# The low half of a weight block, split before or after the background work of its slot

## The chip, the cores and the metric

The kernel runs on one core of one Trainium2 chip. The metric is the device time of one execution in microseconds, from the first to the last instruction of the core and the little that lies around it. The core has five engines with a queue each: TensorE (PE; its weight loads are shown as PEld), VectorE (DVE), ScalarE (ACT), GpSimd (POOL) and SyncE (SP, which here issues the weight transfers).

## The reference

One decoder step in float32, for 512 prompt positions and 8 x 8 sampled ones, 576 rows in all. Attention, convolution and the output projection come first; what the change touches is the MLP and the gate behind them:

```python
    x = x + jnp.concatenate([attn, conv_y], axis=-1) @ w_out
    hid = jnp.square(jax.nn.relu(rms_norm(x, g_mlp) @ w_up))      # 2048 -> 8192
    x = x + hid @ w_down                                          # 8192 -> 2048
    gate = jax.nn.sigmoid(rms_norm(x, g_ple) @ w_ple_gate)        # 2048 -> 2048
    return x + (pe @ w_ple) * gate
```

## The kernel before

**Numbers.** Every float32 operand is split into a high half, rounded to TensorE's fast float32 form, and a low half, the rest. ScalarE makes the high half (`split_hi`, L163), VectorE then the low one from the operand and the high half (`split_lo`, L166). A product is three matmuls: high weights by high rows (L1692), high by low (L1693), low by high (L1694).

**Blocks.** The second phase (`phase2`, from about 963 us on) works through weight blocks, called quads: 2 x 2 tiles of 128 x 128 weights against 2 x 2 tiles of 128 x 288 row operands. In up (256 quads, 32 output pairs p of 8) and down (256 quads, in segments of mostly 7) a quad is not done with 8 tile products but with 7, after Strassen's scheme: three sums of the weights (VectorE, L1918 to L1920) give 7 weight rows, three sums of the row operands (`tsums`, L1778 to L1781, the tile T) give 7 operand rows, and `PRODS` says which weight row meets which operand row for which of the 7 results q0 to q6. So a quad is 7 x 3 = 21 matmuls of 288 columns. The gate (120 quads, `plain`, L1762 to L1764) uses plain products.

**A slot of the loop.** The loop over quads (L1660 to L1723) writes, for quad t, in this order: the second part of the previous segment's end (`combine_tail`, L1817 ff.: VectorE takes the results out of PSUM), `W.prep(t + 2)` (`QStream.prep`: the high split of the block after the next on ScalarE, one pending weight sum, its low split, one more sum), the 21 matmuls, then the background. In the last quad of a segment there is no general background; `combine_head` stands there instead (L1803 ff.: q0 and q4 are copied by ScalarE at L1810 and L1813, then L1811 and L1812 on VectorE use up q5 and q6).

**Background.** Generators wait in queues: `fin_up` (squares the finished up rows: L1447 on VectorE, L1450 and L1451 on ScalarE), `operands` and `tsums` (T), `low_rows` (splits of rows for down, tile lr), `slot` (splits of the next row operands, tile xs: two high splits on ScalarE, two low ones on VectorE), and the gate's end (`fin_gate`, L1500 and L1502). `bg.run(t, dt)` adds an allowance dt of VectorE time and runs steps until it is used up; `bg.wait` only adds it; `flush` runs an item to its end where it is needed. All this happens when the program is written: on the chip each engine runs its queue in the order written.

**What ties the engines.** There are 3 buffers of split weights (w2hl), so the high split of quad t + 2 waits for TensorE to end quad t - 1. There are 4 buffers of raw weights (w2r, two quads each); SyncE's transfer into one waits for the last low split that read it. The 8 PSUM banks turn round: the fourth product of a new segment takes the bank that L1811 frees.

Of the kernel before, what the change touches and what calls it, by code (L numbers as in the profile page):

```python
# [13 lines left out]
ALU = mybir.AluOpType  # L14
# [6 lines left out]
HR = 288  # L21
# [65 lines left out]
def f(ap):  # L87
    return ap.bitcast(F32)


def braid(t, sets=4):
    return t.rearrange("p (b a c) -> p a b c", a=sets, c=4)


def both(t):
    return t[..., 0], t[..., 1]


class Shift:


    def __init__(self, t, off):
        self.t, self.off = t, off
# [6 lines left out]
def EL(n):  # L110

    return n / 960.0 + 0.07


class WStream:
# [24 lines left out]
    def low(self):  # L140
        for c in sorted(set(self.raw) & set(self.hl)):
            hi, lo = self.hl[c]
            self.nc.vector.tensor_tensor(lo, self.raw.pop(c), f(hi), ALU.subtract)  # L143
# [13 lines left out]
class Kern:  # L157
# [1090 lines left out]
    def outproj(self, gen):  # L1248

        nc, a = self.nc, self.a  # L1250
        self.open2()
        bg, t2 = self.bg, self.t2
        for n in range(KT):
            self.on = n
            if n % 2 == 0:
                if n >= 4:
                    bg.flush(self.fin_of[0, n // 2 - 2])
                self.oc_ = t2.tile([128, 2, NR], F32, name="c", tag="c", bufs=3)
            self.rx = self.w2.tile([128, NR], F32, name="rx", tag="t5", bufs=1)
            nc.sync.dma_start(self.rx, a["x"][:, n, :])  # L1260
            h = 6 if n == 0 else 0
            for _ in gen:
                bg.spend(EL(512) / 2)
                if n == KT - 4 and h == 0:
                    for i in range(4):
                        self.W.dma(i)
                if n == KT - 3 and h % 2:
                    bg.spend(self.W.ahead(h // 2))
                if n == KT - 1 and h in (2, 4, 6):
                    bg.spend(self.W.prep(h // 2 - 1))  # L1270
                bg.run(8 * n + h, 1.6)
                h += 1
            if n % 2 and n < KT - 1:
                self.fin_of[0, n // 2] = bg.add(0, self.fin_out(n // 2, self.oc_))
            gen = self.gemm_tile(self.out_evac if n < KT - 2 else self.last_evac)
# [5 lines left out]

    PRODS = ((0, 2, 0), (6, 5, 5), (5, 6, 4), (4, 4, 3), (2, 0, 2), (1, 3, 1), (3, 1, 6))

    def open2(self):

# [144 lines left out]
    def phase2(self):  # L1432
# [11 lines left out]
        V = nc.vector.tensor_tensor  # L1444
# [25 lines left out]
        def rows_of(g):  # L1470
            return {3: (0, 1), 4: (0,), 5: (1,)}[g]
# [81 lines left out]
        segs, W, slots, fin_of = self.segs, self.W, self.slots, self.fin_of  # L1553
# [67 lines left out]
        for n in range(RING, len(seq)):  # L1621
            g, j = seq[n]
# [37 lines left out]
        for t, (si, k) in enumerate(quadlist):  # L1660
            g, p, *_ = segs[si]
            ks = self.orders[si]
            n, i = len(ks), t - seg0[si]
            if prev:
                pg, ppr, c, r, pfinal, pp_ = prev
                if pg >= 3:
                    cost = self.plain_end(ppr, c, rb)
                else:
                    cost = self.combine_tail(ppr, EL)
                    c = c[0]  # L1670
                bg.spend(cost)
                late = (pg, pp_) == (1, 31)
                fin_of[pg, pp_] = bg.add(2 if late else 0, fins[pg](pp_, c, r, pg if pg >= 3 else pfinal))
                if not late:
                    recent.append(fin_of[pg, pp_])
                prev = None
            s = slots[min(g, 3), k]
            if s.work is not None:
                bg.flush(s.work)
                s = slots[min(g, 3), k]  # L1680
            bg.spend(W.prep(t + 2))
            hi, lo = W.hl.pop(t)
            if i == 0:
                pr = {}
            if g >= 3:
                self.plain(pr, hi, lo, s, i == 0, i == n - 1, rows_of(g))
            else:
                for (q, ia, ib) in self.PRODS:
                    if i == 0:
                        pr[q] = self.P_()  # L1690
                    o, xh, xl = braid(pr[q][:, :HR]), braid(s.hi[:, ib, :]), braid(s.lo[:, ib, :])
                    nc.tensor.matmul(o, hi[:, ia, :], xh, start=(i == 0), stop=False)  # L1692
                    nc.tensor.matmul(o, hi[:, ia, :], xl, start=False, stop=False)  # L1693
                    nc.tensor.matmul(o, lo[:, ia, :], xh, start=False, stop=(i == n - 1))  # L1694
            for fn in hooks.get(t, ()):
                fn()
            if g == 2 and p in (4, 5, 6) and i in (0, 2):
                bg.nudge(2)
            slow = p == 0 and g != 2
            if i == (n - 2 if g < 4 else 5) and not slow:  # L1700
                if g > 1:
                    bg.flush_all(0)
                r = pre[g](p, lastseg[g, p] == si)
            dt = (2.79, 3.18, 1.59, 1.59)[max(g - 2, 0)]
            if i == n - 1:
                bg.wait(1000 + t, dt)
            else:
                bg.run(1000 + t, dt)
            if g == 1 and p == 0 and i + 2 < n and slots[1, ks[i + 2]].work:
                bg.flush(slots[1, ks[i + 2]].work)  # L1710
            if i == n - 1:
                if g > 1:
                    bg.flush_all(0)
                if slow:
                    r = pre[g](p, lastseg[g, p] == si)
                if recent[0]:
                    bg.flush(recent[0])
                if g >= 3:
                    c = t2.tile([128, 2, NR], F32, name="c", tag="c", bufs=3)
                else:  # L1720
                    c = self.combine_head(pr, cx if (g, p) == (1, 31) else None)
                    bg.spend(2 * EL(HR))
                prev = (g, pr, c, r, lastseg[g, p] == si, p)  # L1723
# [3 lines left out]
        pg, ppr, c, r, pfinal, p = prev  # L1727
        c, acc = c[:, :, :HR], self.acc2[:, HR:]
# [44 lines left out]
    def tsums(self, T, c):  # L1773

        V = self.nc.vector.tensor_tensor
        b21, b22 = c[:, 1, :HR], c[:, 1, HR:]
        first = c.rearrange("p a (b n) -> p (a b) n", b=2)[:, :2, :]
        V(T[:, 0::2, :], c[:, :, HR:], first, ALU.subtract)  # L1778
        yield 0.67
        V(T[:, 1, :], b22, T[:, 0, :], ALU.subtract)  # L1780
        V(T[:, 3, :], T[:, 1, :], b21, ALU.subtract)  # L1781
        yield 0.74

    def split7(self, s, rp, T):
# [32 lines left out]
    def combine_tail(self, pr, EL):  # L1817
        nc = self.nc
        V = nc.vector.tensor_tensor
        q = lambda i: pr[i][:, :HR]  # L1820
        c, wt = pr["c"]
        c11, c21, c22 = c[:, 0, :HR], c[:, 1, :HR], c[:, 1, HR:]
        V(c11, q(1), c11, ALU.add)
        V(wt[:, 0, :], q(2), wt[:, 1, :], ALU.subtract)
        V(c21, c22, q(3), ALU.subtract)
        V(c[:, :, HR:], c[:, :, HR:], wt, ALU.add)
        return 3 * EL(HR) + EL(2 * HR)


class Slot:  # L1830
    hi = lo = work = None
# [57 lines left out]
class QStream:  # L1889
# [3 lines left out]
    def __init__(self, kern, loads, EL):  # L1893

        self.k, self.nc, self.pool, self.loads, self.EL = kern, kern.nc, kern.w2, loads, EL
        self.where = [(l, i) for l, (_, m, _) in enumerate(loads) for i in range(m)]
        self.raw, self.done, self.hl, self.todo = {}, set(), {}, []

    def dma(self, l):
        if l < len(self.loads) and l not in self.raw:  # L1900
# [33 lines left out]
    def prep(self, q):  # L1934
        if q >= len(self.where) or q in self.hl:
            return 0
        l, i = self.where[q]
        cost = self.sums(l)
        if i == 0:
            self.some(3)  # L1940
            cost += self.sums(l + 1)
            self.dma(l + 3)
        n = 4 if self.loads[l][2] else 7
        w = self.raw[l][:, i, :n]
        t = self.pool.tile([128, 7 * 256], F32R, name="w2hl", tag="w2hl", bufs=3)
        at = 0 if n == 7 else self.GATE_AT
        hi, lo = both(t[:, at:at + n * 256].rearrange("p (a b c) -> p a b c", b=128, c=2))
        self.k.split_hi(hi, w)
        self.some(1)
        self.k.split_lo(lo, w, hi)  # L1950
        self.hl[q] = hi, lo
        self.some(1)
        return cost + self.EL(128 * n)


def quads(w, np_, kp):
# [97 lines left out]
```

## Time and profile before

| | |
|---|---|
| median of 3 runs | 2619.11 us (2618.01 to 2619.18) |
| the profiled execution | 2617.45 us, its span 2615.7 us |
| granted TensorE clock, mean | 0.995 |
| busy: TensorE, VectorE, ScalarE, GpSimd | 2557.8, 2041.6, 1261.3, 529.7 us |
| phase 2 | from about 963 us to the end |

TensorE is busy for 98% of the span, so a view of busy shares says little more than that it is the bound; what is left to win or lose are its waits. Those are told by what released it (a table of waits), and placed by windows: in a window without any wait 789 or 790 matmuls stand in 100 us. Why VectorE or ScalarE came late is then read from their own rows in time. A row of the timeline gives the start, the duration, the engine, the line, what is written from what, the shape, how many instructions it stands for, and in brackets the idle time before it with what ended that. A row of the waits gives total us, times, longest us.

### The profile page before, as it was taken

Reading aid. Unit: us, or ns where it says so; the run is one execution under the profiler, and the core shown is the slowest. Engines: PE = TensorE matmul, PEld = TensorE weight load, DVE = VectorE, ACT = ScalarE, POOL = GpSimd, SP = SyncE. Lnnn points to the kernel's source line nnn. Section 1 sums busy time; section 2 is a strip of 40 time slices with the busy share of each in tenths; the row PEclk is TensorE's granted clock in tenths of the full one; section 3 lists DMA queues with packets and bytes.
Section 4 is the critical chain, followed back from the end, with each engine's and each line's share of the span. In section 5 each row is a group of like instructions: output and inputs, shape, how many; then the busy total and the mean of one; then the engine's idle time right before and its main releaser. Section 6 shows DMA issues by size and latency. Waiting matters only on the chain.

```text
span 2615.7 us, 55774 instructions
## 1 busy us (share of the span) xinstructions
PE 2557.8 (98%) x21910; PEld 2477.1 (95%) x21910; DVE 2041.6 (78%) x3552; ACT 1261.3 (48%) x1714; POOL 529.7 (20%) x942
## 2 busy tenths in 40 slices
PE   9999999999999999999999999999999999999997
PEld 8999999888999999999999999999999999999997
DVE  5577777655665458998899999899888988998676
ACT  5322233235554335555555555655454555555654
POOL 2288777711120000000000000110000000000110
PEclk9999999999999999999999999999999999999998
DMA  6598998999855564444444444777565666656675
GB/s 207 184 316 296 306 301 298 300 311 321 292 191 162 174 201 159 157 151 156 167 161 151 146 152 153 255 189 218 159 199 136 181 174 180 180 189 221 201 245 176
DMA packets 240362, 543.83 MB, mean 208 GB/s; under 512 B 26049, under 2 KB 27074, under 8 KB 240098
## 3 DMA queue, kind: packets, MB, share of 16 engines
q1 hardware_dynamic: 170402, 325.97, 38.5%
q0 software_dynamic: 36160, 153.32, 18.5%
q10 hardware_dynamic: 33536, 60.96, 7.1%
q8 instruction: 172, 2.82, 0.4%
q14 instruction: 92, 0.75, 0.1%
HBM read 445.33 MB, written 94.83 MB: 207 GB/s over the span
## 4 chain that ended last, share of the span: by engine, by line
PE 71%; DVE 15%; DMA 5%; issue 4%; ACT 3%; SPq 0%; ACTq 0%; POOL 0%; DVEq 0%; POOLq 0%
PE U L529 24%; PE P L1692 11%; PE P L1694 11%; PE P L1693 11%; DVE w2hl L166 5%; PE P L1764 2%; PE D L893 2%; PE P L1763 2%; PE P L1762 2%; DMA w2r<-in_w_down 2%; PE O L932 2%; ACT w2hl L163 2%; DVE w2r L1918 1%; DVE xs L166 1%; DVE w2r L1919 1%
## 5 line engine op out<-in xcount | busy, mean ns | idle before, releaser
L1692 PE MATMUL P<-xs,w2hl 128*128 128x288 f32 x3584 | 1044.0, 291 | 14.2 <-DVE c L1811 13.2
L1694 PE MATMUL P<-xs,w2hl 128*128 128x288 f32 x3584 | 1037.6, 290 | 5.2 <-DVE w2hl L166 4.8
L1693 PE MATMUL P<-xs,w2hl 128*128 128x288 f32 x3584 | 1034.8, 289 | 4.2 <-DVE xs L166 4.0
L163 ACT ACTIVATE w2hl<-w2r 128x896 fp32r<-128x896 f32 (+1 forms) x632 | 642.4, 1026 | 672.4 <-PE P L1694 333.9
L166 DVE TENSOR_TENSOR w2hl<-w2r,w2hl 128x896 fp32r<-128x896 f32 (+1 forms) x632 | 643.8, 1021 | 171.5 <-ACT w2hl L163 170.2
L1692 PEld LDWEIGHTS P<-xs,w2hl 128*128 128x128 f32 x3584 | 708.7, 198 | 21.4 <-DVE c L1811 17.8
L1693 PEld LDWEIGHTS P<-xs,w2hl 128*128 128x128 f32 x3584 | 712.4, 199 | 6.0 <-DVE xs L166 5.3
L1694 PEld LDWEIGHTS P<-xs,w2hl 128*128 128x128 f32 x3584 | 707.7, 197 | 9.0 <-DVE w2hl L166 8.7
L529 PE MATMUL U<-xh,whl 128*128 128x288 f32 x3584 | 647.2, 295 | 2.7 <-ACT xh L163 2.7
L529 PEld LDWEIGHTS U<-xh,whl 128*128 128x128 f32 x3584 | 527.3, 195 | 21.5 <-issue 16.1
L529 PE MATMUL U<-xl,whl 128*128 128x288 f32 x1792 | 374.6, 290 | 1.1 <-DVE xl L357 0.8
L137 ACT ACTIVATE whl<-wraw 128x512 fp32r<-128x512 f32 x224 | 157.9, 706 | 348.0 <-PE U L529 304.0
L529 PEld LDWEIGHTS U<-xl,whl 128*128 128x128 f32 x1792 | 287.7, 195 | 2.2 <-DVE xl L357 2.1
L143 DVE TENSOR_TENSOR whl<-wraw,whl 128x512 fp32r<-128x512 f32 x224 | 161.0, 719 | 116.5 <-ACT whl L137 116.1
L1081 DVE SCALAR_TENSOR_TENSOR y<-ue,cv,y 128x512 f32<-128x512 f32 x240 | 182.9, 762 | 5.3
L1918 DVE TENSOR_TENSOR w2r<-w2r 128x512 f32<-128x512 f32 (+1 forms) x273 | 178.0, 652 | 11.4 <-DMA w2r<-in_w_down 11.4
L1082 POOL TENSOR_SCALAR cvt<-us,cv 128x64 f32<-128x64 f32 x240 | 165.0, 688 | 22.3
L1764 PE MATMUL P<-xs,w2hl 128*128 128x288 f32 x512 | 148.5, 290 | 2.0 <-DVE w2hl L166 2.0
L1763 PE MATMUL P<-xs,w2hl 128*128 128x288 f32 x512 | 147.8, 289 | 1.1 <-DVE xs L1601 1.1
L1762 PE MATMUL P<-xs,w2hl 128*128 128x288 f32 x512 | 148.3, 290 | 0.0
L1920 DVE TENSOR_TENSOR w2r<-w2r 128x256 f32<-128x256 f32 (+1 forms) x273 | 111.3, 408 | 7.5
L1386 POOL DMA_DIRECT2D di<-c x31 | 16.9, 545 | 481.5 <-ACT c L1451 481.5
(409 smaller groups left out, 2662.8 us busy)
## 6 DMA issues: line engine op xcount, KB each, us to landing
k<-in_cache_kv SPq DMA_DIRECT2D x256, 256.0 KB, 4.3
v<-in_cache_kv SPq DMA_DIRECT2D x256, 256.0 KB, 4.5
w2r<-in_w_up SPq DMA_DIRECT2D x127, 512.0 KB, 3.9
w2r<-in_w_down SPq DMA_DIRECT2D x112, 512.0 KB, 3.9
wraw<-in_w_main ACTq DMA_DIRECT2D x156, 256.0 KB, 4.8
xs<-di POOLq DMA_DIRECT2D x32, 1008.0 KB, 6.4
w2r<-in_w_gate SPq DMA_DIRECT2D x60, 512.0 KB, 5.1
x<-c POOLq DMA_DIRECT2D x48, 576.0 KB, 5.8
```

Source lines behind the costliest of these rows:

```text
L163: self.nc.scalar.activation(out, in_, AF.Copy, **kw)
L166: self.nc.vector.tensor_tensor(out, in_, f(hi), ALU.subtract)
L529: self.nc.tensor.matmul(braid(u[:, r, :HR]), w, braid(x[:, r * HR:(r + 1) * HR]), start=first and n == 0, stop=last and n == 2)
L1081: nc.vector.scalar_tensor_tensor(y, ue[:, j:j + NPR], w, y, ALU.mult, ALU.add)
L1082: nc.gpsimd.tensor_scalar(t, us[:, :, j:j + 8], w, None, ALU.mult)
L1692: nc.tensor.matmul(o, hi[:, ia, :], xh, start=(i == 0), stop=False)
L1693: nc.tensor.matmul(o, hi[:, ia, :], xl, start=False, stop=False)
L1694: nc.tensor.matmul(o, lo[:, ia, :], xh, start=False, stop=(i == n - 1))
L1762: nc.tensor.matmul(o, hi[:, ia, :], xh, start=first and kh == 0, stop=False)
L1763: nc.tensor.matmul(o, hi[:, ia, :], xl, start=False, stop=False)
L1764: nc.tensor.matmul(o, lo[:, ia, :], xh, start=False, stop=last and kh == 1)
L1918: lambda: V(w[:, :, 4:6, :], w[:, :, 0:1, :].broadcast_to([128, m, 2, 128]), w[:, :, 1:3, :], ALU.add),
```

## The change

Four parts:

1. The low split of a weight block and the weight sum behind it leave `prep` and become `QStream.low`, which is called behind the background of the slot (in the output projection right behind `prep`).
2. In `PRODS` (result, weight row, operand row), the results q6 and q5 of the second and third product change places, and the weight rows 5 and 6 with them. The operand rows are read in the same turn as before (0, 5, 4, 3, 2, 1, 6), but T's second and third row, which are operand rows 4 and 5, have changed their content with each other, so that the first sum writes two rows next to each other.
3. The background's allowances dt go from 2.79, 3.18, 1.59, 1.59 to 2.67, 3.06, 1.53, 1.53.
4. In `combine_tail` the subtraction with q2 stands before the addition with q1.

```diff
@@ outproj
                 if n == KT - 1 and h in (2, 4, 6):
                     bg.spend(self.W.prep(h // 2 - 1))
+                    self.W.low()
                 bg.run(8 * n + h, 1.6)
@@
-    PRODS = ((0, 2, 0), (6, 5, 5), (5, 6, 4), (4, 4, 3), (2, 0, 2), (1, 3, 1), (3, 1, 6))
+    PRODS = ((0, 2, 0), (5, 6, 5), (6, 5, 4), (4, 4, 3), (2, 0, 2), (1, 3, 1), (3, 1, 6))
@@ phase2
-            dt = (2.79, 3.18, 1.59, 1.59)[max(g - 2, 0)]
+            dt = (2.67, 3.06, 1.53, 1.53)[max(g - 2, 0)]
             if i == n - 1:
                 bg.wait(1000 + t, dt)
             else:
                 bg.run(1000 + t, dt)
+            W.low()
@@ tsums
-        V(T[:, 0::2, :], c[:, :, HR:], first, ALU.subtract)
+        V(T[:, :2, :], c[:, :, HR:], first, ALU.subtract)
         yield 0.67
-        V(T[:, 1, :], b22, T[:, 0, :], ALU.subtract)
-        V(T[:, 3, :], T[:, 1, :], b21, ALU.subtract)
+        V(T[:, 2, :], b22, T[:, 0, :], ALU.subtract)
+        V(T[:, 3, :], T[:, 2, :], b21, ALU.subtract)
@@ combine_tail
+        V(wt[:, 0, :], q(2), wt[:, 1, :], ALU.subtract)
         V(c11, q(1), c11, ALU.add)
-        V(wt[:, 0, :], q(2), wt[:, 1, :], ALU.subtract)
@@ QStream.prep
         self.k.split_hi(hi, w)
         self.some(1)
-        self.k.split_lo(lo, w, hi)
         self.hl[q] = hi, lo
-        self.some(1)
+        self.rest = w, hi, lo
         return cost + self.EL(128 * n)
+
+    def low(self):
+        if self.rest:
+            w, hi, lo = self.rest
+            self.k.split_lo(lo, w, hi)
+            self.some(1)
+            self.rest = None
```

How the instructions stand at two places. The first is in up, pair 11, on VectorE. Names: `w2r` raw weights and their sums (L1918 to L1920 before, L1920 to L1922 in the change), `w2hl` the low split of a block, `T` the sums of the row operands, `lr` the low split of T. Before:

```order
L1920 TENSOR_TENSOR w2r<-w2r 128x2x128
L166 TENSOR_TENSOR w2hl<-w2r,w2hl 128x896
L1778 TENSOR_TENSOR T<-c 128x2x288
L1780 TENSOR_TENSOR T<-c,T 128x288
L1781 TENSOR_TENSOR T<-T,c 128x288
L1918 TENSOR_TENSOR w2r<-w2r 128x2x256
L166 TENSOR_TENSOR w2hl<-w2r,w2hl 128x896
```

and with the change:

```order
L1922 TENSOR_TENSOR w2r<-w2r 128x2x128
L1780 TENSOR_TENSOR T<-c 128x576
L1782 TENSOR_TENSOR T<-c,T 128x288
L1783 TENSOR_TENSOR T<-T,c 128x288
L166 TENSOR_TENSOR w2hl<-w2r,w2hl 128x896
L1920 TENSOR_TENSOR w2r<-w2r 128x2x256
L166 TENSOR_TENSOR w2hl<-w2r,w2hl 128x896
```

T's three instructions now stand ahead of the first of the two low splits. The second place is in down, on VectorE, where the row operands of a coming quad are built (`xs`). Before:

```order
L166 TENSOR_TENSOR w2hl<-w2r,w2hl 128x896
L1919 TENSOR_TENSOR w2r<-w2r 128x128
L1920 TENSOR_TENSOR w2r<-w2r 128x128
L166 TENSOR_TENSOR w2hl<-w2r,w2hl 128x896
L166 TENSOR_TENSOR xs<-xs 128x864
L166 TENSOR_TENSOR xs<-xs 128x1152
L1918 TENSOR_TENSOR w2r<-w2r 128x2x256
```

and with the change:

```order
L166 TENSOR_TENSOR w2hl<-w2r,w2hl 128x896
L1921 TENSOR_TENSOR w2r<-w2r 128x128
L1922 TENSOR_TENSOR w2r<-w2r 128x128
L166 TENSOR_TENSOR xs<-xs 128x864
L166 TENSOR_TENSOR xs<-xs 128x1152
L166 TENSOR_TENSOR w2hl<-w2r,w2hl 128x896
L1920 TENSOR_TENSOR w2r<-w2r 128x2x256
```

The two low splits of the row operands have passed the low split of the weights. ScalarE's order there is the same before and after; it makes the high split of the weights first and the two of the row operands behind it:

```order
L163 ACTIVATE w2hl<-w2r 128x896 x4
L163 ACTIVATE xs<-xs 128x864
L163 ACTIVATE xs<-xs 128x1152
L163 ACTIVATE w2hl<-w2r 128x896 x3
L1810 ACTIVATE c<-P 128x288
```

TensorE's order differs only in the names of the products.

More of the change, by code (lines that the diff above doesn't have):

```diff
@@ L1896, in __init__ @@
         self.where = [(l, i) for l, (_, m, _) in enumerate(loads) for i in range(m)]
-        self.raw, self.done, self.hl, self.todo = {}, set(), {}, []
+        self.raw, self.done, self.hl, self.todo, self.rest = {}, set(), {}, [], None
     def dma(self, l):
```

## The prediction

> **What bounds the kernel now.** I read the page's busy shares first.
>
> ```profile
> PE 2557.8 (98%) x21910; PEld 2477.1 (95%) x21910; DVE 2041.6 (78%) x3552; ACT 1261.3 (48%) x1714; POOL 529.7 (20%) x942
> ```
>
> TensorE has 98% of the span of 2615.7 us. The change adds and removes no matmul, so it can act only through TensorE's waits. Second view: those waits, by what ended them (total us, times, longest).
>
> ```profile
> PE P L1692 <- DVE c L1811: 13.2, 17, 1.9
> PE P L1694 <- DVE w2hl L166: 4.8, 11, 1.0
> PE P L1693 <- DVE xs L166: 4.0, 6, 1.2
> PE P L1764 <- DVE w2hl L166: 2.0, 3, 1.5
> ```
>
> L1811 is VectorE's first instruction of the segment's end (`combine_head`): it frees the PSUM bank that the fourth product of the next segment takes. L166 is the low split, of weights (w2hl) or of row operands (xs); L1764 is the gate's matmul. Third view, windows: us, busy time (x instructions) of PE, PEld, DVE, ACT, POOL, then the granted clock, DMA share, GB/s. Four are in up, the last in the gate.
>
> ```profile
> 1200.00:1300.00 100.00, 97.63 (x748) 96.03 (x749) 91.37 (x144) 55.84 (x63) 9.18 (x17) 1.00 0.49 164
> 1300.00:1400.00 100.00, 98.88 (x768) 98.00 (x767) 91.04 (x143) 55.13 (x58) 9.71 (x18) 1.00 0.49 161
> 1400.00:1500.00 100.00, 100.00 (x790) 100.00 (x789) 90.33 (x142) 55.28 (x58) 6.46 (x12) 1.00 0.44 141
> 1500.00:1600.00 100.00, 100.00 (x789) 100.00 (x789) 89.65 (x142) 54.02 (x57) 8.09 (x15) 1.00 0.45 155
> 2540.00:2580.00 40.00, 40.00 (x317) 39.88 (x316) 28.87 (x49) 24.40 (x39) 6.78 (x10) 1.00 0.82 286
> ```
>
> Full pace is 790 matmuls in 100 us, 0.1266 us each, at a granted clock of 1.00; a quad of 21 is then 2.66 us. 1400 to 1600 has nothing to win. 1200 to 1400 falls 42 + 22 = 64 matmuls short, 64 x 0.1266 = 8.1 us, which is an upper bound since some matmul records may be missing; the idle time alone is 2.37 + 1.12 = 3.5 us, the lower one. Fourth view: VectorE's own waits from 957 us on.
>
> ```profile
> DVE w2hl L166 <- ACT w2hl L163: 170.2, 194, 3.3
> DVE w2r L1918 <- DMA w2r<-in_w_down: 11.4, 6, 2.7
> ```
>
> So VectorE stands 170 us with a low split at its head that waits for ScalarE's high split, while background work is ready behind it. The change turns that order round. It pays only where TensorE then waits less.
>
> **Up, pairs 9 to 16: a gain.** Here the background also makes the low rows (lr) for down. Around quad 94 (VectorE, ScalarE, TensorE; start, duration, in brackets the idle time before):
>
> ```profile
> 1238.79 1.10 DVE L166 TENSOR_TENSOR w2hl<-w2r,w2hl 128x896 fp32r<-128x896 f32 x1 [1.15 <-ACT w2hl L163]
> 1239.80 0.75 DVE L1778 TENSOR_TENSOR T<-c 128x576 f32<-128x576 f32 x1
> 1241.08 0.46 DVE L1781 TENSOR_TENSOR T<-T,c 128x288 f32<-128x288 f32 x1
> 1243.74 1.10 DVE L166 TENSOR_TENSOR w2hl<-w2r,w2hl 128x896 fp32r<-128x896 f32 x1 [1.60 <-ACT w2hl L163]
> ...
> 1241.57 1.17 ACT L163 ACTIVATE lr<-T 128x1152 fp32r<-128x1152 f32 x1 [2.81 <-DVE T L1781]
> 1242.65 2.02 ACT L163 ACTIVATE w2hl<-w2r 128x896 fp32r<-128x896 f32 x2
> ...
> 1244.15 0.29 PE L1693 MATMUL P<-xs,w2hl 128*128 128x288 f32 x1
> 1244.89 0.40 PE L1694 MATMUL P<-xs,w2hl 128*128 128x288 f32 x1 [0.46 <-DVE w2hl L166]
> ```
>
> The chain is T on VectorE, lr on ScalarE, then the next high split, its low split, and TensorE: 0.74 us between two matmuls instead of 0.13. The three T instructions take from 1239.80 to 1241.54. In the changed order they fill the idle 1.15 us and start at 1237.64; T is ready about 2 us earlier, and so are lr, the high split and the low split at 1243.74. The matmul was 0.6 us late, so the stall goes. The twelve stalls of this kind, all between 1199 and 1360 us, come by the starts of the matmuls to 0.42 to 0.94 us each and 7.7 us together, inside the bounds 3.5 and 8.1. Against them, a low split that now stands behind an lr split gets late by about 0.26 us in four quads, 1.1 us. Term: **-6.6**.
>
> **Up, pairs 17 to 31: nothing, narrowly.** The costliest move is fin_up's multiplication (L1447) ahead of the low split:
>
> ```profile
> 1514.59 1.10 DVE L166 TENSOR_TENSOR w2hl<-w2r,w2hl 128x896 fp32r<-128x896 f32 x1
> 1515.93 1.35 DVE L1447 TENSOR_TENSOR c<-c,rb 128x1152 f32<-128x1152 f32 x1
> 1517.20 0.41 DVE L1920 TENSOR_TENSOR w2r<-w2r 128x256 f32<-128x256 f32 x1
> ...
> 1517.10 0.29 PE L1694 MATMUL P<-xs,w2hl 128*128 128x288 f32 x1
> ```
>
> The low split ends at 1515.69; 1.27 us later (from L1447's start to its successor's) it ends at 1516.96, and the matmul that reads it starts at 1517.10. It fits by 0.14 us. Term 0; if it just misses, I take 0.11 us for each of some 23 such quads, 2.5 us.
>
> **Down: a loss.** In twelve segments a row operand's `slot` build stands in quad 3 of 7, behind the low split of quad 5. Quads count from 0. The splits of the first and the last of the twelve:
>
> ```profile
> 1869.60 1.11 DVE L166 TENSOR_TENSOR w2hl<-w2r,w2hl 128x896 fp32r<-128x896 f32 x1 [1.04 <-ACT w2hl L163]
> ...
> 2235.87 1.12 DVE L166 TENSOR_TENSOR w2hl<-w2r,w2hl 128x896 fp32r<-128x896 f32 x1 [0.85 <-ACT w2hl L163]
> ```
>
> ScalarE, VectorE and TensorE at the tenth:
>
> ```profile
> 2197.94 1.99 ACT L163 ACTIVATE xs<-xs 128x864 fp32r<-128x864 f32 x2
> 2203.98 2.10 ACT L163 ACTIVATE w2hl<-w2r 128x896 fp32r<-128x896 f32 x2 [3.04 <-DVE w2r L1920]
> ...
> 2196.93 0.29 DVE L1920 TENSOR_TENSOR w2r<-w2r 128x128 f32<-128x128 f32 x1
> 2198.07 1.11 DVE L166 TENSOR_TENSOR w2hl<-w2r,w2hl 128x896 fp32r<-128x896 f32 x1 [0.85 <-ACT w2hl L163]
> 2199.09 2.32 DVE L166 TENSOR_TENSOR xs<-xs 128x864 fp32r<-128x864 f32 x2
> 2201.32 0.69 DVE L1918 TENSOR_TENSOR w2r<-w2r 128x512 f32<-128x512 f32 x1
> 2207.91 0.45 DVE L1811 TENSOR_TENSOR c<-c,P 128x288 f32<-128x288 f32 x1
> ...
> 2208.51 0.31 PE L1692 MATMUL P<-xs,w2hl 128*128 128x288 f32 x1
> ```
>
> ScalarE's order stays: high split of the weights, then the two high splits of the rows. Now VectorE has the weights' low split first, which covers the time of the first row split on ScalarE. In the changed order the rows' low splits come first, and the first of them needs its own high split, which ends at 2197.94 + 0.91 = 2198.85, not 2198.07. That such a split does wait for ScalarE is seen at the start of phase 2:
>
> ```profile
> 978.10 2.42 DVE L166 TENSOR_TENSOR xs<-xs 128x864 fp32r<-128x864 f32 x2 [0.86 <-ACT xs L163]
> ...
> 977.14 1.99 ACT L163 ACTIVATE xs<-xs 128x864 fp32r<-128x864 f32 x2 [1.71 <-DMA xs<-ui]
> ```
>
> By hand: first row split 2198.9 to 2199.9; the second needs the high split that ends at 2199.93 and runs to 2201.25; the weights' low split to 2202.35, overlapping; the sum L1918 at 2202.26 instead of 2201.32. That is +0.94 us for all that is queued behind on VectorE: sums, two more low splits, then L1811. Nothing soaks it up. ScalarE's next high split (2203.98) itself waits for VectorE's sum L1920, so the idle time between moves along with the chain. L1811 ends at 2208.36, and its matmul starts 0.15 us later, at 2208.51, already held a little. So TensorE loses 0.94 us per segment, 12 x 0.94 = **+11.3**. It cannot be under zero there (nothing in such a segment comes earlier); the upper bound is the whole high split ahead plus a handover, some 1.2 us, or 14.
>
> On this the Trainium skill, "PSUM — Partial Sum Buffer", section "Engine vs sequencer instructions", says that the queues of ScalarE, VectorE and GpSimd are strictly first in, first out. It speaks against this change here: whatever is put ahead of the low split holds it and all sums behind it until ScalarE has delivered. The trace agrees (the 0.86 us at 978.10); by the rule the sum would be the same +0.94.
>
> **The odd places in down, and the start.** Of the six late weight transfers in the waits above, four lie ahead of segment ends whose own delay takes up the build (left out of the twelve). Other builds that move ahead of a split without cover cost about 0.9 (first segments), 0.8 (around 2262 us) and 1.5 (two builds of gate rows); one at the end of up 0.3; the start and the norm of the rows 0.5, a loss of 1.6 there being won back by 1050 us. Sum +4.0. Gains: before two segment ends the build moves behind the sums and fills VectorE's idle 0.7 us, and two smaller ones win 0.4 and 0.7: -2.4. These are my readings of single places like the one above; I give the group ±4.
>
> **Transfers.** SyncE's load into a weight buffer waits for the low split that last read it, so some now start later, by 2.3 us behind a build.
>
> ```profile
> w2r<-in_w_down SPq DMA_DIRECT2D x112, 512.0 KB, 3.9
> ```
>
> A load lands 3.9 us after its issue and holds two quads, 5.3 us of work; it is issued about two loads before its sums, so 2.3 us more is covered. At the six late ones no background stands ahead of that split. Term 0; were one of the six 2.3 us later, TensorE would lose up to 2.3.
>
> **Gate.** The background's pair L1500, L1502 moves ahead of a split:
>
> ```profile
> 2542.10 0.74 DVE L1500 TENSOR_TENSOR c<-c,rp 128x576 f32<-128x576 f32 x1
> 2545.95 0.70 DVE L166 TENSOR_TENSOR w2hl<-w2r,w2hl 128x512 fp32r<-128x512 f32 x1 [1.09 <-ACT w2hl L163]
> ```
>
> The squares on ScalarE, which stand ahead of that high split, start about 1.3 us earlier, and TensorE's low-split stalls of the gate shrink: 2.0 us of waits in the table above, up to 4.5 with the pauses right behind them. Between 0 and -4.5 I take **-1.5**, as most of them are near the segment ends, whose background stays.
>
> **Products and row layout.** The swap of products 2 and 3 with T's rows moves no row operand in the order of reading; only the weight rows 5 and 6 change places. The bound: 317 matmuls in 40 us in the gate are 126.2 ns each, against 126.6 in up. If that whole difference hung on the order, it would be 0.4 ns x 21 x 512 = 4.3 us either way. I take 0, since the operands that stream come in the same order. The Trainium skill ("TensorE: Matmul & The Clock Gate", "Step-by-step: what each phase is for") makes the gap between matmuls N cycles and about 2.5 ns; for 288 columns that is an estimate of 122.5 ns whatever the order, and so also 0 for the swap, though 126.6 here shows something more in the gap.
>
> The T instruction writes two rows next to each other in place of two apart (0.75 us, off the path); the tail's swap of two subtractions frees two banks 0.4 us earlier or later that no matmul waits for. The smaller allowances move a few background steps one quad on, which is in the order from which the terms above are read: 0.
>
> **Sum:** -6.6 + 0 + 11.3 + 4.0 - 2.4 - 1.5 = +4.8 us on the profiled execution's 2617.45. That run lies 1.66 us below the median 2619.11, so on the median: **2623.9 us**, 0.18% slower. About 0.2%, 5.2 us, is what a measurement of this kernel tells from no change; the forecast lies at that edge.
>
> **Rivals.**
> *The builds cost nothing* (a gain). VectorE idles 0.85 us at 2198.07 and more later; if the segment has slack before L1811, the 0.94 vanishes: 4.8 - 11.3 = -6.5, 2612.6. For it: VectorE is 78% busy. Against: L1811's end and its matmul lie 0.15 us apart. It decides if the waits on L1811 in those segments stay as they are.
> *Steady up starts to stall* (slower). The 0.14 us of room in pairs 17 to 31 is less than the scatter of a handover. If VectorE comes 0.3 us later there, some 23 quads lose 0.1 to 0.4 us, 2.5 to 9, middle 6: 2629.9. It decides once the low split ends past 1517.05 in the scale above. Against it: one instruction's duration hardly varies.
> *The layout does what its words say* and closes the 0.4 ns: 4.8 - 4.3, 2619.6, no change. Against: the streaming order is the same.
>
> **Chances.** Forecast 0.48 (its own range 2619 to 2629), builds free 0.22, steady up stalls 0.18, layout 0.12. Faster by over 0.2%: nearly all of the second, 0.20. Slower: the third and some 0.22 of the forecast, 0.40. Within: 0.40. Range 2612 to 2631: from the second case to just above the third's middle.
>
> **What would show it.** Waits for L1811's successor (two lines further down) near 1 us in the segments about 1879, 1898, 1917, 2035, 2208; VectorE's waits of xs L166 for ScalarE up from a few to some 15, 1.7 us each at the builds; no waits of L1694 between 1200 and 1360; windows 1400 to 1600 still at 789 to 790 matmuls. Wrong would be: unchanged ends of segments in down, or stalls in 1400 to 1600.

## The result

The changed kernel takes 2641.49 us (median of 4 runs, 2640.2 to 2643.45), the kernel before beside it 2619.14 us: a ratio of 1.0094 (95% interval 1.0081 to 1.0106), 22 us slower. The profiled execution has a span of 2638.5 us against 2615.7. The forecast was 2623.9 us with a range up to 2631: the right side, a fifth of the size.

Where it went, by the starts of the first matmuls of up, of down and of the gate and of the gate's last (us):

| | before | changed | difference | forecast |
|---|---|---|---|---|
| ahead of up | 980.8 | 978.6 | -2.2 | 0 |
| up | 701.4 | 698.3 | -3.1 | -5.8 |
| down | 712.3 | 738.9 | +26.6 | +12.1 |
| gate | 203.1 | 205.1 | +2.0 | -1.5 |
| behind the gate | 18.1 | 17.6 | -0.5 | 0 |

The line numbers of the changed kernel lie a little further down: L1692 to L1694 are now L1693 to L1695, L1811 is L1813, the weight sums are L1920 to L1922, T is L1780 to L1783. TensorE's waits in the changed kernel (total us, times, longest), to be set against the four rows of before:

```profile
PE P L1695 <- DVE w2hl L166: 14.8, 25, 1.9
PE P L1693 <- DVE c L1813: 14.0, 24, 1.0
PE P L1766 <- DVE w2hl L166: 3.0, 3, 1.8
PE P L1694 <- DVE xs L166: 2.7, 5, 0.7
```

The waits for a weights' low split have tripled (4.8 to 14.8 us, 11 to 25 times); the segments' ends wait 24 times instead of 17. VectorE's own waits from 957 us on:

```profile
DVE w2hl L166 <- ACT w2hl L163: 129.3, 187, 3.3
DVE xs L166 <- ACT xs L163: 41.4, 22, 3.6
DVE w2r L1920 <- DMA w2r<-in_w_down: 5.2, 3, 2.5
```

and in the kernel before the row that answers to the second of these:

```profile
DVE xs L166 <- ACT xs L163: 3.9, 4, 2.5
```

The change did what its words say to the first row: 170 us became 129. But 37.5 of the 41 us came back in the second row. VectorE waits as long as before (about 170 us), now at the row operands' splits, and with a weights' split and the sums queued behind.

The windows of up and the one in the gate (PE, PEld, DVE, ACT, POOL busy, clock, DMA share, GB/s):

```profile
1200.00:1300.00 100.00, 99.56 (x778) 98.94 (x778) 94.84 (x148) 57.70 (x64) 9.40 (x18) 1.00 0.52 168
1300.00:1400.00 100.00, 99.85 (x784) 99.62 (x783) 91.95 (x146) 56.29 (x60) 9.15 (x17) 1.00 0.52 164
1400.00:1500.00 100.00, 100.00 (x784) 99.86 (x783) 90.92 (x141) 54.20 (x55) 8.05 (x15) 1.00 0.47 150
1500.00:1600.00 100.00, 100.00 (x786) 99.93 (x785) 89.57 (x140) 54.10 (x57) 6.45 (x12) 1.00 0.44 138
2540.00:2580.00 40.00, 39.52 (x307) 39.03 (x306) 32.85 (x64) 23.58 (x39) 9.67 (x16) 1.00 0.76 265
```

From 1200 to 1400 TensorE idles 0.6 us in place of 3.5: the gain in up is there. From 1400 to 1600 it still counts as 100% busy, but 9 matmuls fewer stand there (1570 for 1579): a loss that the busy share doesn't show. (The gate's window lies at another place of the gate than before, 21 us earlier in its work, since the gate starts that much later.)

**The place in down**, the same segment as in the forecast: ScalarE, VectorE, TensorE.

```profile
2207.06 1.08 ACT L163 ACTIVATE w2hl<-w2r 128x896 fp32r<-128x896 f32 x1 [1.33 <-PE P L1695]
2208.14 1.99 ACT L163 ACTIVATE xs<-xs 128x864 fp32r<-128x864 f32 x2
...
2207.09 0.29 DVE L1922 TENSOR_TENSOR w2r<-w2r 128x128 f32<-128x128 f32 x1
2209.11 2.42 DVE L166 TENSOR_TENSOR xs<-xs 128x864 fp32r<-128x864 f32 x2 [1.73 <-ACT xs L163]
2211.44 1.09 DVE L166 TENSOR_TENSOR w2hl<-w2r,w2hl 128x896 fp32r<-128x896 f32 x1
2219.04 0.44 DVE L1813 TENSOR_TENSOR c<-c,P 128x288 f32<-128x288 f32 x1
...
2218.82 0.29 PE L1695 MATMUL P<-xs,w2hl 128*128 128x288 f32 x1
2219.53 0.41 PE L1693 MATMUL P<-xs,w2hl 128*128 128x288 f32 x1 [0.43 <-DVE c L1813]
2219.78 0.29 PE L1694 MATMUL P<-xs,w2hl 128*128 128x288 f32 x1
```

The row split waits 1.73 us for ScalarE where the weights' split had waited 0.85, as worked out. From the end of L1922 to the start of the segment's end are 11.66 us (2207.38 to 2219.04) instead of 10.69 (2197.22 to 2207.91): +0.97, forecast +0.94. TensorE's step at the segment's end is 0.71 us instead of about 0.13, and the next one 0.25.

**The place in up**, quad 94 again:

```profile
1235.49 0.76 DVE L1780 TENSOR_TENSOR T<-c 128x576 f32<-128x576 f32 x1 [0.16 <-ACT c L1452]
1237.15 1.10 DVE L166 TENSOR_TENSOR w2hl<-w2r,w2hl 128x896 fp32r<-128x896 f32 x1
1239.45 1.10 DVE L166 TENSOR_TENSOR w2hl<-w2r,w2hl 128x896 fp32r<-128x896 f32 x1 [0.60 <-ACT w2hl L163]
...
1237.27 1.18 ACT L163 ACTIVATE lr<-T 128x1152 fp32r<-128x1152 f32 x1 [0.84 <-DVE T L1783]
```

T fills the idle time, lr starts at 1237.27 instead of 1241.57, and the low split that had come 0.6 us late ends 1.4 us ahead of its matmul. (This trace is 2.3 us ahead here, so lr came 2.0 us earlier relative to TensorE; forecast 2.)

**Steady up.** L1448 is fin_up's multiplication, now ahead of the split:

```profile
1508.51 1.35 DVE L1448 TENSOR_TENSOR c<-c,rb 128x1152 f32<-128x1152 f32 x1
1509.78 1.09 DVE L166 TENSOR_TENSOR w2hl<-w2r,w2hl 128x896 fp32r<-128x896 f32 x1
...
1510.83 0.29 PE L1694 MATMUL P<-xs,w2hl 128*128 128x288 f32 x1
1510.96 0.38 PE L1695 MATMUL P<-xs,w2hl 128*128 128x288 f32 x1
1511.17 0.30 PE L1693 MATMUL P<-xs,w2hl 128*128 128x288 f32 x1
```

The split ends at 1510.87, the matmul that reads it starts at 1510.96, on time, but the next one comes 0.21 us later instead of 0.127: 0.09 us lost without a wait in the tables above, in 19 quads of the pairs 4 to 31, about 2 us. TensorE's weight loads (PEld) at this place show where they go:

```profile
1510.71 0.20 PEld L1694 LDWEIGHTS P<-xs,w2hl 128*128 128x128 f32 x1
1510.92 0.20 PEld L1695 LDWEIGHTS P<-xs,w2hl 128*128 128x128 f32 x1
```

At full pace a load begins 0.12 us ahead of its matmul (1510.71 for the matmul at 1510.83). The load of the split weights was thus due at 1510.83, ahead of the split's end; it begins at 1510.92, 0.05 us behind that end and 0.09 us late.

### The profile page after: what moved, and what is told of

Same layout as the page of the kernel before. It is cut to its first block, busy times and chain, and to the rows that moved or that the text cites. A ratio compares the mean times of both kernels' runs of the same rounds, so it can differ in the third digit from the quotient of the medians.

```text
span 2638.5 us, 55956 instructions
## 1 busy us (share of the span) xinstructions
PE 2568.6 (97%) x21910; PEld 2479.7 (94%) x21910; DVE 2049.2 (78%) x3552; ACT 1259.9 (48%) x1714; POOL 529.8 (20%) x942
## 4 chain that ended last, share of the span: by engine, by line
PE 65%; DVE 15%; issue 11%; DMA 6%; ACT 3%; SPq 0%; ACTq 0%; POOL 0%; DVEq 0%; POOLq 0%
PE U L529 23%; PE P L1695 9%; PE P L1693 9%; PE P L1694 9%; DVE w2hl L166 4%; PE P L1766 2%; PE P L1765 2%; PE P L1764 2%; PE D L893 2%; PE O L932 2%; DVE xs L166 2%; DMA xs<-di 1%; ACT w2hl L163 1%; DMA w2r<-in_w_down 1%; DVE w2r L1920 1%
## 5 line engine op out<-in xcount | busy, mean ns | idle before, releaser
L1695 PE MATMUL P<-xs,w2hl 128*128 128x288 f32 x3584 | 1044.6, 291 | 16.5 <-DVE w2hl L166 14.8
L1693 PE MATMUL P<-xs,w2hl 128*128 128x288 f32 x3584 | 1045.4, 292 | 15.2 <-DVE c L1813 14.0
L1694 PE MATMUL P<-xs,w2hl 128*128 128x288 f32 x3584 | 1036.0, 289 | 3.2 <-DVE xs L166 2.7
L1695 PEld LDWEIGHTS P<-xs,w2hl 128*128 128x128 f32 x3584 | 708.3, 198 | 26.9 <-DVE w2hl L166 26.2
L1693 PEld LDWEIGHTS P<-xs,w2hl 128*128 128x128 f32 x3584 | 709.6, 198 | 24.5 <-DVE c L1813 19.2
L1694 PEld LDWEIGHTS P<-xs,w2hl 128*128 128x128 f32 x3584 | 712.9, 199 | 4.7 <-DVE xs L166 3.8
L1920 DVE TENSOR_TENSOR w2r<-w2r 128x512 f32<-128x512 f32 (+1 forms) x273 | 177.9, 652 | 5.2 <-DMA w2r<-in_w_down 5.2
L1922 DVE TENSOR_TENSOR w2r<-w2r 128x256 f32<-128x256 f32 (+1 forms) x273 | 111.6, 409 | 9.3
```

Source lines behind the costliest of these rows:

```text
L1920: lambda: V(w[:, :, 4:6, :], w[:, :, 0:1, :].broadcast_to([128, m, 2, 128]), w[:, :, 1:3, :], ALU.add),
```

## The experiments

Three theories were set against each other. L: the later place of the low split makes the loss, mostly in down, where row splits wait for ScalarE. D: the smaller allowances make it. P: the new order of products and rows makes it. In the diffs, "after" is the changed kernel.

**Allowances (e1).** After, with one line back:

```diff
-            dt = (2.67, 3.06, 1.53, 1.53)[max(g - 2, 0)]
+            dt = (2.79, 3.18, 1.59, 1.59)[max(g - 2, 0)]
```

> The changed kernel with the old allowances dt (2.79, 3.18, 1.59, 1.59). Theory L (the later place of the low split makes the loss): the same as the changed kernel within 3 us, 2638 to 2644 us. Theory D (the smaller allowances, which move background steps one quad on, make it): most of the 22 us comes back, below 2627 us. Theory P (the new order of products and rows makes it): as L.

2643.72 us, ratio 1.0085 (1.0064 to 1.0106); down takes 739.4 us. As slow as the change: D falls.

**Products alone (e2).** Before, with the new `PRODS`, `tsums` and `combine_tail`, as in the change's diff.

> The kernel before with the new order of products, the new layout of T and the swapped subtraction in the segment's tail, and nothing else. Theory L: 2619 us within 3 us. Theory P: at least a third of the loss, above 2626 us, with a longer time between matmuls at the second and third product (130 to 131 ns at the third and fourth matmul before).

2620.57 us, ratio 1.0008 (0.9997 to 1.0019): not told from no change, so P falls as the cause of the 22 us. In its trace down is longer (716.5 us). One thing there is systematic: the fifth product of a segment starts 0.18 to 0.19 us after the matmul ahead of it instead of 0.127, waiting for L1812, which now frees its bank later; in down some 26 times 0.055, 1.4 us. It stands in the changed kernel's trace as well, about as often. The longer time at the third and fourth matmul of a quad stayed as it was.

**Late in up only (e3).** After, with

```diff
             bg.spend(W.prep(t + 2))
+            if g > 1:
+                W.low()
```

> The changed kernel, but in down and in the gate the low split stands ahead of the background again; in up it stays behind it. Theory L: all of down's loss (26.6 us between the first matmuls of down and of the gate) goes, up's gain of 3 to 5 us stays: 2613 to 2617 us, clearly faster than before. Theories D and P: still above 2630 us.

2614.81 us, ratio 0.9990 (0.9980 to 1.0001); up 697.9 us, down 714.3, gate 203.3. Down's loss is gone and up's gain is kept (3.5 us). L holds; "clearly faster" was too much.

**Late in down only (e8)**, and **in the gate only (e10).** Before (old products, layout, allowances), with `low` behind the background only where g is 2, or only where g is over 2.

> The kernel before, where in down alone the low split goes behind the background (up, gate, products, layout and allowances as before). If down's loss stands by itself: 22 to 28 us above the kernel before, 2640 to 2646 us. If it needs the other parts of the change: below 2632 us.

2640.55 us, ratio 1.0091 (1.0076 to 1.0106); down takes 738.4 us, 26.1 more than before. Down's loss stands by itself. VectorE's waits for its row splits (second row) are about those of the changed kernel; the first row includes up, which is as before here:

```profile
DVE w2hl L166 <- ACT w2hl L163: 157.3, 177, 3.3
DVE xs L166 <- ACT xs L163: 43.6, 22, 4.1
```

> The kernel before, where in the gate alone the low split goes behind the background. If the 2.0 us that the changed kernel's gate takes longer come from this: the time from the first to the last matmul of the gate goes from 203.1 us to 204.5 to 206 us, and the whole by 1 to 3 us. If it was the forecast's gain that other parts of the change undid: under 202.5 us.

2617.91 us, ratio 0.9998 (0.9987 to 1.0009); the gate takes 204.7 us. With the gate untouched the other traces have 203.1 to 204.8 us, so the forecast's gain of 1.5 isn't there, and whether there is a loss of 1 or 2 us can't be told.

**The low split ahead of row builds only (e4).** After, in `slot` and in the gate's row build:

```diff
             self.split_hi(hi[:, i:i + n, :], r)
+            self.W.low()
             self.split_lo(lo[:, i:i + n, :], r, hi[:, i:i + n, :])
```

> The changed kernel, but the low split of the weights is issued ahead of the low splits of the next row operands (slot builds, and the gate's row builds), and stays behind all other background. Theory L with the mechanism of the forecast (row splits wait on ScalarE and hold the weights' low split and the sums): nearly all of down's loss goes, 2616 to 2624 us, and VectorE's waits of row splits for ScalarE fall from 41 us to under 10. If the loss is that any background ahead of the low split makes it late: above 2632 us.

2621.14 us, ratio 1.0007 (0.9998 to 1.0017); down takes 719.2 us. Its waits of VectorE:

```profile
DVE w2hl L166 <- ACT w2hl L163: 142.1, 205, 3.3
DVE xs L166 <- ACT xs L163: 5.3, 6, 2.6
```

So 20 of the 26.6 us that down lost hang on row builds standing ahead of the weights' split and of the sum that moves with it (no run parts these two); against e3's 714.3 us, 5 us of the loss remain. Is it that the builds wait for ScalarE, or that they are work?

**Row high splits one quad earlier (e5).** After, with `slot` as

```diff
+        for i, n in ((0, 3), (3, 4)):
+            self.split_hi(hi[:, i:i + n, :], f(lo[:, i:i + n, :]))
+        yield -1
         for i, n in ((0, 3), (3, 4)):
-            r = f(lo[:, i:i + n, :])
-            self.split_hi(hi[:, i:i + n, :], r)
-            self.split_lo(lo[:, i:i + n, :], r, hi[:, i:i + n, :])
+            self.split_lo(lo[:, i:i + n, :], f(lo[:, i:i + n, :]), hi[:, i:i + n, :])
             yield EL(n * HR)
```

> The changed kernel, but a row operand's two high splits on ScalarE are issued one quad ahead of its two low splits on VectorE; all low splits of the weights stay behind the background. If the loss in down is VectorE's wait for ScalarE at the row splits: near the 2621 us of the run that put the weights' split ahead of the builds, 2616 to 2626 us. If it is the 2.3 us of row work itself standing ahead of the weights' low split: above 2634 us.

2623.74 us, ratio 1.0018 (1.0009 to 1.0027); down takes 723.2 us. The row work (2.3 us) still stands ahead of a weights' low split, a quad later, and 16 of the 20 us are gone. Quad by quad, the twelve segments of the forecast cost 1.2 us more than in the trace of before, where the other traces with down's split early (e2, e3, e6, e10) have 1.1 to 3.3 us more: nothing of their loss is left. So there the wait for ScalarE makes the loss, and not the work. What is left stands mostly around the builds of the gate's rows (quads 480 to 505), 3.2 us more than in e4's trace; this run leaves those builds as they are in the changed kernel, and they still wait 1.3 to 1.4 us for ScalarE, three times.

**A better kernel (e6).** Before, with `low` behind the background in up alone, but called ahead of the steps that made quads late (here `fin_up`; likewise ahead of `low_rows`' splits of c and of the row splits):

```diff
+            W.low()
             V(c, c, rbb, ALU.mult)
```

> The kernel before (old products, layout, allowances), where in up alone the low split goes behind the background, except that it stays ahead of the multiplication L1447, of the row splits, and of the low rows of c. So T and the first low rows go ahead, and what made quads late by 0.1 us (steady up) and 0.43 us (four quads of the pairs 10 to 16) does not. By the gains read from the trace of the changed kernel (5 us in the pairs 9 to 16, without 2 + 1.7 us of losses): 6 to 8 us below the kernel before. If the losses are traded for new ones elsewhere: 2 to 4 us below, as with everything late in up.

2609.74 us, ratio 0.9969 (0.9957 to 0.9981): faster than both kernels, by 8 us. Up takes 693.1 us, 8.3 less than before; down and gate are as before.

**Using the idle time before the segments' ends (e7, e9).** As e6 in up; in down late too, but ahead of the gate's row splits and of the addition in down's end (`fin_down`), and `slot` with the high splits a quad ahead and a pause behind each low split (in e9 `slot` so in down alone):

```diff
             yield EL(n * HR)
+            yield -1
```

> As e6 in up; in down the low split of the weights goes behind the background too, but a row operand's high splits come one quad ahead, and its two low splits stand in two quads, the second in VectorE's idle 0.7 us before the segment's end. If VectorE's chain sets the waits at the segments' ends (about 12 us in down): 4 to 6 us below e6, 10 to 14 us below the kernel before. If those waits have another cause: the same as e6.

> e7, but only down's row operands have their high splits a quad ahead and their low splits apart; up's are as in e6. e7's trace lost 1.7 us against e6 at the first builds of up and won 3.5 us in down. If both stand by themselves: 2 to 5 us below e6, that is 11 to 15 us (0.4 to 0.6%) below the kernel before. If the gain in down is scatter: like e6, 8 to 10 us below.

e7: 2609.16 us, ratio 0.9965 (0.9952 to 0.9978). e9: 2609.81 us, ratio 0.9968 (0.9955 to 0.9980). Neither can be told from e6: the expected 4 to 6 us (e7) and 2 to 5 us (e9) were missed. TensorE's waits of e9, then VectorE's for transfers:

```profile
PE P L1701 <- DVE w2hl L166: 8.2, 10, 2.0
PE P L1699 <- DVE c L1828: 6.5, 9, 1.0
...
DVE w2r L1935 <- DMA w2r<-in_w_down: 13.9, 6, 2.9
```

The waits at the segments' ends did fall, to 6.5 us (11.5 in e6), so VectorE's chain does set them in part, by 0.2 to 1.2 us at each of some 16 segments. But quad by quad against e6's trace, the segments that end at about 1952, 2106 and 2257 us lose 2.7, 2.6 and 1.6 us; they are ones whose weight transfers come late in the kernel before too. The rest of the gain is taken there, as waits for a low split (8.2 us). Why a segment ahead of a late transfer pays for the earlier ones was not looked into further.

## Why the prediction was wrong

**Bound, right.** Nothing but TensorE's waits moved the time; the granted clock was 0.997 against 0.995.

**Up, pairs 9 to 16, right with a small miss.** The twelve stalls are gone, 7.7 us by the starts of the matmuls, as forecast. The four new ones cost 0.43 us each, 1.7 for 1.1. Net -6.0 for -6.6.

**Steady up, the condition was right and the term wrong.** The split came in time by 0.09 us where 0.14 were worked out, and that was not enough: 0.1 us in 19 quads, 2 us. The room was counted to the matmul, and its weight load begins 0.12 us ahead of it. The text named this price (0.11 us, 2.5 us) and took 0, taking "ahead of the matmul" for "without cost".

**Twelve builds, the mechanism right, the price near.** Against the trace of before they cost 14.3 us for 11.3, 1.2 us per segment for 0.94; against the trace of e3, which has the changed kernel's products and down's split early, 11.8 us. In the tenth VectorE's chain was late by 0.97 us as worked out; VectorE did nothing behind the waiting row split until it was released, as the Trainium skill has it ("PSUM — Partial Sum Buffer", "Engine vs sequencer instructions"); the 1.73 us agree. Counted from TensorE's start of quad 5, the segment's end on VectorE (L1811, now L1813) came 0.88 to 1.29 us later than in the trace of before in eleven segments and 1.97 us in one, 13.4 us in all. TensorE lost 0.05 to 0.14 us more than that in each. The sum had left this out: behind a late matmul the next step is longer too (2219.53 to 2219.78 is 0.25 us for 0.127). In such a segment two matmuls come late, one for the weights' split and one at the end; they share the delay.

**The odd places, the step that failed.** They were forecast at +3.2 and -2.4 in down, +0.8 together, and came to about +12.3 (12.8 against e3's trace). The span of the changed kernel lies 18 us above the forecast, and 11.5 of them are here. Worst was the sentence that a build moving behind the sums "fills VectorE's idle 0.7 us" before two segment ends, a gain of 1.3 us. The first of them, in the kernel before (the idle 0.7 us) and then in the changed one:

```profile
1972.76 2.32 DVE L166 TENSOR_TENSOR xs<-xs 128x864 fp32r<-128x864 f32 x2
...
1976.71 1.11 DVE L166 TENSOR_TENSOR w2hl<-w2r,w2hl 128x896 fp32r<-128x896 f32 x1 [0.70 <-ACT w2hl L163]
```

```profile
1975.03 1.09 ACT L163 ACTIVATE w2hl<-w2r 128x896 fp32r<-128x896 f32 x1 [2.09 <-DVE w2r L1922]
1975.99 1.97 ACT L163 ACTIVATE xs<-xs 128x864 fp32r<-128x864 f32 x2
...
1976.94 2.41 DVE L166 TENSOR_TENSOR xs<-xs 128x864 fp32r<-128x864 f32 x2 [1.48 <-ACT xs L163]
1979.27 1.08 DVE L166 TENSOR_TENSOR w2hl<-w2r,w2hl 128x896 fp32r<-128x896 f32 x1
```

ScalarE makes the weights' high split first, which itself waits for VectorE's sums (L1922), and only then the rows'. So the row split can't run in the idle 0.7 us; it waits 1.48, and the matmul that reads the weights' split starts 0.56 us late. These two cost 2.0 us instead of gaining 1.3. It is the same wait that the text had worked out for the twelve, not applied here. With the high splits a quad earlier (e5) the two did gain, 2.2 us: the idle time could be used once ScalarE was not in the way. The quads just behind the previous ends (356, 357, 412, 413), where single row splits now stand ahead, cost another 1.6 and were not counted. The builds of the gate's rows and what stands around them cost about 4 us for 1.5, the first segments 1.4 us (against e3's trace) to 2.8 us (against before's) for 0.9. That row builds as a class are the cause is shown by e4. The shares of the single places are read from traces; those of e1 and e8 have about the same: 1.6 and 1.5 us at the two segment ends, 1.4 and 1.6 behind the previous ones, 4.7 and 4.3 around the gate's rows.

**Gate, wrong.** Forecast -1.5; 203.1 to 205.1 us in the trace, 204.7 with the gate alone. TensorE's waits for a low split in the gate did not shrink (3.0 us for 2.0); the stalls moved. Steps of 1.76 and 0.49 us at the gate's matmuls 254 and 278 became one of 2.11 at 242, and 0.62 at 1046 became 0.78 at 986; e10's trace has 2.11 and 0.77 at the same two. The forecast had taken it that they would shrink; why others came was not looked into.

**Products and layout, and allowances, near.** 0 was forecast for both. The allowances can't be told from 0. The products have 1.4 us at the fifth product in the trace, and their run alone lies 2 us above before (ratio 1.0008), with no change in its interval. The swap of weight rows had no effect on the pace, as forecast.

**Transfers, right:** VectorE's waits for them fell (11.4 to 5.2 us). That is probably because VectorE came later to its sums; it was not tested.

**The rivals.** "The builds cost nothing" is refuted (e8, e4). "Steady up starts to stall" was right in kind, with 2 us just under its lower end. The layout closed no gap. None of them had what decided: the forecast's own mechanism at more places than twelve.

## What to carry to other kernels

Where an engine works in order, moving an instruction that waits behind other work paid only if that work didn't wait for the same third engine: T's sums needed from ScalarE only what was nearly done (they waited 0.2 us at most, 1.6 in all) and won, the row splits needed a later instruction of ScalarE and lost. Count every place where the new order puts a waiting instruction ahead, not only the regular ones: the irregular ones made nearly half of down's loss. And move selectively: the same move held to up, with the split ahead of the steps that had made quads late there (e6), is 0.3% faster than before, where the change everywhere is 0.9% slower.

## What the runs showed of the hardware that was not expected

A matmul that waits for its operand makes the next one late as well: it starts 0.25 us behind the late one instead of 0.127 (1244.89, then 1245.14, in the trace of before; 2219.53, then 2219.78, in that of after). Its weight load is late with it: in both places it is shown to start with the matmul, where at full pace it starts 0.12 us ahead, and the step is longer by just that. And an operand that is ready 0.09 us ahead of its matmul's start still costs such a longer step (1510.96, then 1511.17), with TensorE shown as 100% busy in its window, since its load was 0.09 us late. The table of matmul waits therefore shows too little. It also counts a wait from the modelled end of the matmul ahead, 0.29 us after its start, and not from the turn of the next one, 0.127 us after it: of the 0.58 us lost at 2219.53 it shows 0.43. Its three rows for up and down add up to 22.0 us before and 31.5 after, 9.5 more, while up and down together lost 23.5 by the starts of the matmuls. The page's rows of weight loads come nearer:

```profile
L1692 PEld LDWEIGHTS P<-xs,w2hl 128*128 128x128 f32 x3584 | 708.7, 198 | 21.4 <-DVE c L1811 17.8
L1693 PEld LDWEIGHTS P<-xs,w2hl 128*128 128x128 f32 x3584 | 712.4, 199 | 6.0 <-DVE xs L166 5.3
L1694 PEld LDWEIGHTS P<-xs,w2hl 128*128 128x128 f32 x3584 | 707.7, 197 | 9.0 <-DVE w2hl L166 8.7
```

```profile
L1695 PEld LDWEIGHTS P<-xs,w2hl 128*128 128x128 f32 x3584 | 708.3, 198 | 26.9 <-DVE w2hl L166 26.2
L1693 PEld LDWEIGHTS P<-xs,w2hl 128*128 128x128 f32 x3584 | 709.6, 198 | 24.5 <-DVE c L1813 19.2
L1694 PEld LDWEIGHTS P<-xs,w2hl 128*128 128x128 f32 x3584 | 712.9, 199 | 4.7 <-DVE xs L166 3.8
```

Their waits for VectorE are 31.8 us before (first three) and 49.2 after, 17.4 more. A forecast made from the matmuls' table should add, as an estimate from these places, about 0.16 us and 0.12 us for each late operand.
